# Up projections with the activations stationary, turned through memory and convolved a strip later

## The chip, the cores and the metric

The kernel runs on one core of a Trainium2 chip. The metric is the device time of one execution in microseconds (us), as a median over runs. Engines are named as in the profile: PE is TensorE's matmul and PEld its weight load, DVE is VectorE, ACT is ScalarE, POOL is GpSimd and SP is SyncE. Time in the trace counts from the first instruction of the profiled execution.

## What is computed

A decoder trunk of two layers on 256 tokens of width 2048. Each layer has attention, a gated feed-forward block with a short causal convolution, and a gated embedding that is added. The change lies in the feed-forward block:

```python
def causal_depthwise_conv(u, w, bias):      # width 3, each channel on its own
    ...
    return y + bias.astype(u.dtype)

def conv_ffn(h, w_up, conv_w, conv_b, w_down):
    u = causal_depthwise_conv(h @ w_up, conv_w, conv_b)
    gate, val = u[..., :D_FF], u[..., D_FF:]
    return (jax.nn.silu(gate) * val) @ w_down
```

`h` is 256 x 2048, `w_up` is 2048 x 11264 (D_FF is 5632) and `w_down` is 5632 x 2048. A token's convolved value takes in the two tokens before it, of the same channel. All data are float32; a product is made of three products of rounded parts, because each operand is split into a high part and the low rest (high x high, high x low, low x high).

## The kernel before

**Weights.** A weight matrix is cut into strips of 512 output columns. `weights` (L286) brings a strip in by SP's queue, 1 MB (four blocks of 128 rows) at a time, into four `raw` buffers, and splits two blocks at once: ACT writes the high part `whi` (L314), DVE the low part `wlo` (L315). Four `whi` and four `wlo` buffers exist, each for two blocks (a pair), so the split of a pair waits until PE has finished the pair four places earlier. An up strip has 16 blocks, which is 8 pairs.

**Two ways to multiply.** `strip_t` (L332) holds 128 x 128 pieces of the weights as the stationary operand and streams the activations. For each block and each of the strip's four groups of 128 channels it makes one matmul of 512 columns (the high weights by both parts of all 256 tokens, L341) and one of 256 columns (the low weights by the high part, L344). Its result lies in four PSUM banks with the channels on the partitions. `strip_v` (L347) holds 128 tokens of the activations as the stationary operand and streams the weights. For each block and each half of the tokens it makes three matmuls of 512 columns (L356 to L358). Its result lies in two PSUM banks with the tokens on the partitions. The banks come from a pool of five (`acc`). Both keep the last two blocks for the end, and then finish one bank after the other.

**The feed-forward block.** `ffn` (L617) calls `part` (L628) for 5 strip pairs, then the down projection of these with `strip_v` (`add_strips`, L595 to L615), then `part` for the other 6, and the down projection again. A strip pair is a strip of gates and the strip of values that they multiply: 22 up strips in each of two layers, 44 in all, each by `strip_t`. After a strip `conv` (L620) takes the four banks: `evac` (L361) adds the two halves of a bank on ACT and DVE (L363, L364) and multiplies by the norm's row `rstd` (L366); ACT scales by the third tap and adds the bias (L624); DVE adds the two other taps, shifted by one and by two tokens (L625, L626). Tokens lie along the free axis here, so a shift is a shift of addresses. Then SiLU on ACT for a gate (L636), or the product with the gate on DVE (L642) and the split into `g` (L152, L153) for a value. The parts `g` feed the down projection in the order of the strips.

**Turning.** The output projections of attention and the gated embeddings use `strip_v` as well and need their sums with channels on the partitions. For three strips of four `turn` (L242) does it: DVE transposes blocks of 32 x 32 (L250), POOL's queue writes them to a scratch tensor in device memory (`there`, L253) and reads them back in another order (`turned`, L257). It is used 15 times. The result has the shape 128 x 8 x 4 x 32: eight runs of 32 tokens for each of four channel groups. It has one buffer.

**Order.** The frame's scheduler puts each engine's instructions in order. `tc.high_priority` draws the weight splits ahead by a fixed distance, and `tc.issue_after` keeps one instruction behind another. Each engine runs its instructions strictly in that order, so one that waits holds all behind it.

Of the kernel before, what the change touches and what calls it, by code (L numbers as in the profile page):

```python
# [13 lines left out]
I32 = mybir.dt.int32  # L14
# [59 lines left out]
def tile_trunk(ctx, tc, head_d, xT_d, x_d, pT_d, pos_d, vec_d, cst_d, csb_d, wqkv, wo_a, wkv, wq_b, wo_b, wup, wdn, wpg, wpp, gfin_d, out_d):  # L74
# [133 lines left out]
    class Norm:  # L208
# [17 lines left out]
        def done(self, row=True):  # L226
# [6 lines left out]
            dg = tt("diag", tag="t", bufs=6)  # L233
# [8 lines left out]
    def turn(s):  # L242

        there = dram.tile([2 * P, 512], F32, tag="turn", name=nm("there"))
        for t in range(2):
            y = rt("y")
            nc.vector.transpose(  # L250
                y.rearrange("p (b o r) -> p o b r", b=4, o=4), strip_of(t, s).rearrange("p (o b c) -> p o b c", o=4, b=4)
            )
            nc.gpsimd.dma_start(there[t * P : (t + 1) * P], y)  # L253
        z = tt("turned", (P, 8, 4, 32), bufs=1)
        back = there.rearrange("(a c) (b f) -> b c a f", c=32, b=4)
        for b in range(4):
            nc.gpsimd.dma_start(z[32 * b : 32 * b + 32].rearrange("p a o r -> p a (o r)"), back[b])  # L257
        return [z[:, :, o] for o in range(4)]
# [27 lines left out]
    def weights(W, s, n, fine=False, before=lambda k0: None, block=None, base=0, ringed=0):  # L286

        size = 2 if fine else RAW
        for k0 in range(0, n, size):
# [8 lines left out]
            for i in range(0, w, 2):  # L298
# [11 lines left out]
                for c in (slice(0, 1), slice(1, 2)) if one else (slice(0, 2),):  # L310
                    r = raw[:, i + c.start : i + c.stop]
                    with tc.high_priority(offset=AHEAD):
                        with tc.issue_after(block(c.start)) if one else ExitStack():
                            last["high"] = nc.scalar.activation(hi[:, c], r, AF.Copy).ins  # L314
                        nc.vector.tensor_tensor(lo[:, c], r, f32(hi[:, c]), op=OP.subtract)  # L315
# [91 lines left out]
    def rotary_angles():  # L407
        pi = tt("posi", (ROT, S), I32, tag="t", bufs=6)
# [5 lines left out]
        n = tt("rn", (ROT, S), tag="t", bufs=6)  # L414
        nh = tt("rnh", (ROT, S), F32R, tag="t", bufs=6)
        nl = tt("rnl", (ROT, S), tag="t", bufs=6)
# [20 lines left out]
    def rotate(t):  # L437

        sw = tt("sw", (ROT, S), tag="t", bufs=6)
# [177 lines left out]
    def ffn(i, xs, rstd):  # L617
        cv = V_CONV + i * 4 * 2 * FB

        def conv(j, ps, y):  # L620
            col = lambda r: vec[:, cv + r * 2 * FB + j : cv + r * 2 * FB + j + 1]
            u = tt("u", tag="t", bufs=6)
            evac(ps, rstd, u)
            nc.scalar.activation(y, u, AF.Identity, scale=col(2), bias=col(3))  # L624
            nc.vector.scalar_tensor_tensor(y[:, 1:], u[:, : S - 1], col(1), y[:, 1:], op0=OP.mult, op1=OP.add)  # L625
            nc.vector.scalar_tensor_tensor(y[:, 2:], u[:, : S - 2], col(0), y[:, 2:], op0=OP.mult, op1=OP.add)  # L626

        def part(strips):  # L628
            gs = []
            for s in strips:  # L630
                ps = strip_t(wup[i], s, xs)
                gates = []
                for o in range(4):
                    y = tt("gate", bufs=4)
                    conv(4 * s + o, ps[o], y)
                    silu = nc.scalar.activation(y, y, AF.Silu).ins  # L636
                    gates.append(y)
                ps = strip_t(wup[i], FB // 4 + s, xs)
                for o in range(4):
                    y = tt("val", tag="t", bufs=6)  # L640
                    conv(FB + 4 * s + o, ps[o], y)
                    nc.vector.tensor_tensor(y, y, gates[o], op=OP.mult)  # L642
                    g = rt("g", dt=F32R)
                    split(y, g)
                    gs.append(g)
            return gs, silu
# [119 lines left out]
    for i in range(2):  # L766
        norm = Norm()
        h = add_strips(wo_a if i == 0 else wo_b, o, G_FFN + i * KB, norm)
        rstd, _ = norm.done()
        pb = p_blocks(i)  # L770
        h, norm = ffn(i, h, rstd)
# [93 lines left out]
```

## Time and profile before

| | |
|---|---|
| median of 3 runs | 2358.26 us (2357.72 to 2359.83) |
| profiled execution | 2358.29 us, of which the span from first to last instruction is 2356.5 us |
| PE busy | 2342.1 us (99%) in 12138 matmuls |
| DVE busy | 1578.5 us (67%) |
| ACT busy | 1270.9 us (54%) |
| POOL busy | 52.4 us (2%) |
| DMA | 458.55 MB, mean 195 GB/s |
| granted TensorE clock | 0.998 of full speed |

The span is the kernel, and what lies around it is 1.8 us. A busy share is that of a whole program with stages of different kinds, so the stage of the up strips is read by windows of its own. The end of a matmul in the trace is modelled, and matmuls overlap in it; the time that one takes is read from the distance between starts.

### The profile page before, as it was taken

Reading aid. Unit: us, or ns where it says so; the run is one execution under the profiler, and the core shown is the slowest. Engines: PE = TensorE matmul, PEld = TensorE weight load, DVE = VectorE, ACT = ScalarE, POOL = GpSimd, SP = SyncE. Lnnn points to the kernel's source line nnn. Section 1 sums busy time; section 2 is a strip of 40 time slices with the busy share of each in tenths; the row PEclk is TensorE's granted clock in tenths of the full one; section 3 lists DMA queues with packets and bytes.
Section 4 is the critical chain, followed back from the end, with each engine's and each line's share of the span. In section 5 each row is a group of like instructions: output and inputs, shape, how many; then the busy total and the mean of one; then the engine's idle time right before and its main releaser. Section 6 shows DMA issues by size and latency. Waiting matters only on the chain.

```text
span 2356.5 us, 31193 instructions
## 1 busy us (share of the span) xinstructions
PE 2342.1 (99%) x12138; PEld 1992.0 (85%) x12138; DVE 1578.5 (67%) x2407; ACT 1270.9 (54%) x1834; POOL 52.4 (2%) x94
## 2 busy tenths in 40 slices
PE   9999999999999999999999999999999999999998
PEld 7888888888888888888888888888888888888886
DVE  7566556778755777755668875677875577775555
ACT  6555545656534556545565444565653455654554
POOL 0000001000000000001010000100000000000100
PEclk9999999999999999999999999999999999999999
DMA  8455456555555555566565544665555555556663
GB/s 297 175 180 173 174 196 220 195 186 190 193 190 190 196 181 195 187 208 230 206 227 193 179 151 171 223 210 181 195 187 191 194 193 184 194 184 211 232 205 117
DMA packets 70133, 458.55 MB, mean 195 GB/s; under 512 B 8640, under 2 KB 9056, under 8 KB 18016
## 3 DMA queue, kind: packets, MB, share of 16 engines
q1 hardware_dynamic: 62352, 434.93, 52.9%
q0 software_dynamic: 5280, 15.73, 2.3%
q10 hardware_dynamic: 2352, 5.88, 0.7%
q8 instruction: 95, 1.56, 0.3%
q14 instruction: 54, 0.44, 0.1%
HBM read 446.56 MB, written 9.96 MB: 194 GB/s over the span
## 4 chain that ended last, share of the span: by engine, by line
PE 98%; DVE 1%; ACT 0%; DMA 0%; issue 0%; SPq 0%; DVEq 0%; ACTq 0%
PE acc L341 36%; PE acc L344 18%; PE accv L357 14%; PE accv L356 14%; PE accv L358 14%; PE two L385 2%; PE two L459 0%; DVE wlo L315 0%; DMA raw<-in_wqkv 0%; ACT whi L314 0%; PE keys L385 0%; PE two L460 0%; ACT sq L216 0%; PE two L267 0%; PE nrm L237 0%
## 5 line engine op out<-in xcount | busy, mean ns | idle before, releaser
L315 DVE TENSOR_TENSOR wlo<-raw,whi 128x1024 fp32r<-128x1024 f32 (+1 forms) x821 | 1002.1, 1221 | 698.2 <-ACT whi L314 694.2
L314 ACT ACTIVATE whi<-raw 128x1024 fp32r<-128x1024 f32 (+1 forms) x821 | 868.2, 1058 | 866.1 <-PE accv L358 425.7
L341 PE MATMUL acc<-h,whi 128*128 128x512 f32 x3712 | 1166.7, 396 | 2.1 <-DVE h L147 1.7
L344 PEld LDWEIGHTS acc<-h,wlo 128*128 128x128 f32 x3712 | 696.6, 188 | 163.9
L344 PE MATMUL acc<-h,wlo 128*128 128x256 f32 x3712 | 730.6, 278 | 0.0
L341 PEld LDWEIGHTS acc<-h,whi 128*128 128x128 f32 x3712 | 566.7, 189 | 5.0 <-DVE h L147 1.9
L356 PE MATMUL accv<-whi,g 128*128 128x512 f32 x704 | 273.9, 389 | 0.0
L357 PE MATMUL accv<-wlo,g 128*128 128x512 f32 x704 | 273.9, 389 | 0.0
L358 PE MATMUL accv<-whi,g 128*128 128x512 f32 x704 | 273.9, 389 | 0.0
L356 PE MATMUL accv<-whi,h 128*128 128x512 f32 x464 | 181.5, 391 | 0.0
L357 PE MATMUL accv<-wlo,h 128*128 128x512 f32 x464 | 181.2, 391 | 0.0
L358 PE MATMUL accv<-whi,h 128*128 128x512 f32 x464 | 181.2, 390 | 0.0
L358 PEld LDWEIGHTS accv<-whi,g 128*128 128x128 f32 x704 | 132.1, 188 | 27.4
L356 PEld LDWEIGHTS accv<-whi,g 128*128 128x128 f32 x704 | 132.1, 188 | 27.4
L357 PEld LDWEIGHTS accv<-wlo,g 128*128 128x128 f32 x704 | 132.1, 188 | 27.2
L363 ACT ACTIVATE c<-acc 128x256 f32<-128x256 f32 x232 | 86.2, 374 | 33.0 <-PE acc L344 32.9
L358 PEld LDWEIGHTS accv<-whi,h 128*128 128x128 f32 x464 | 87.1, 188 | 18.0
L356 PEld LDWEIGHTS accv<-whi,h 128*128 128x128 f32 x464 | 87.1, 188 | 17.7
L357 PEld LDWEIGHTS accv<-wlo,h 128*128 128x128 f32 x464 | 87.1, 188 | 17.4
L364 DVE TENSOR_TENSOR c<-acc,c 128x256 f32<-128x256 f32 x232 | 91.6, 415 | 0.0
L357 PE MATMUL accv<-wlo,o 128*128 128x512 f32 x224 | 87.4, 390 | 0.0
L358 PE MATMUL accv<-whi,o 128*128 128x512 f32 x224 | 87.3, 390 | 0.0
(184 smaller groups left out, 1457.7 us busy)
## 6 DMA issues: line engine op xcount, KB each, us to landing
raw<-in_wup SPq DMA_DIRECT2D x176, 1024.0 KB, 4.8
raw<-in_wdn SPq DMA_DIRECT2D x88, 1024.0 KB, 4.8
raw<-in_wqkv SPq DMA_DIRECT2D x44, 1024.0 KB, 4.8
raw<-in_wpg SPq DMA_DIRECT2D x32, 1024.0 KB, 5.1
raw<-in_wkv SPq DMA_DIRECT2D x24, 1024.0 KB, 4.8
raw<-in_wo_a SPq DMA_DIRECT2D x16, 1024.0 KB, 4.8
raw<-in_wq_b SPq DMA_DIRECT2D x12, 1024.0 KB, 4.9
raw<-in_wo_b SPq DMA_DIRECT2D x12, 1024.0 KB, 4.8
```

The lines of the kernel that those rows point to most:

```text
L314: last["high"] = nc.scalar.activation(hi[:, c], r, AF.Copy).ins
L315: nc.vector.tensor_tensor(lo[:, c], r, f32(hi[:, c]), op=OP.subtract)
L341: nc.tensor.matmul(ps[o], hi[:, c], xs[k], start=k == 0, stop=False)
L344: nc.tensor.matmul(ps[o][:, S:], lo[:, c], xs[k][:, :S], start=False, stop=k == n - 1)
L356: nc.tensor.matmul(ps[t], xl, hi, start=k == 0, stop=False)
L357: nc.tensor.matmul(ps[t], xh, lo, start=False, stop=False)
L358: nc.tensor.matmul(ps[t], xh, hi, start=False, stop=k == n - 1)
L363: last["copy"] = nc.scalar.activation(c, ps[:, S:], AF.Copy).ins
L364: last["sum"] = nc.vector.tensor_tensor(c, ps[:, :S], c, op=OP.add).ins
L385: run.append(nc.tensor.matmul(*args, skip_group_check=True, **kw).ins)
```

## The change

All up strips but the last value strip of each part go by `strip_v`: 9 of 10 strips in a first part and 11 of 12 in a second, 40 in the two layers. A strip's two banks are copied by ACT with the norm's column `rc` as scale (two copies of 128 x 512), transposed by DVE in 32 x 32 blocks, written to device memory and read back by POOL's queue. `turn` is cut for this into `turn_out` and `turn_in`. The convolution of a strip is issued one strip later, behind the next strip's copies and transposes. It works on runs of 32 tokens (`conv_turned`): for each channel group one ACT instruction and two DVE instructions inside the runs, then four small DVE instructions that carry the last one or two tokens of a run into the next. SiLU and the product with the gate are done for the four channel groups at once. The last value strip of a part stays with `strip_t` and the old `conv`; the gates of the same pair are convolved during it. Some buffers move: the transposes' output leaves the ring for the buffers `eh` and `el`, the tag `t` has 3 buffers and not 6, `gate` and `val` have one buffer of 128 x 4 x 256 each.

```diff
-    def turn(s):
+    def turn_out(strips):
         there = dram.tile([2 * P, 512], F32, tag="turn", name=nm("there"))
-        for t in range(2):
-            y = rt("y")
-            nc.vector.transpose(
-                y.rearrange("p (b o r) -> p o b r", b=4, o=4), strip_of(t, s).rearrange("p (o b c) -> p o b c", o=4, b=4)
-            )
+        for t, strip in enumerate(strips):
+            y = tt("y", (P, 768), tag=("eh", "el")[t], bufs=1)[:, :512]
+            last["turned"] = nc.vector.transpose(
+                y.rearrange("p (b o r) -> p o b r", b=4, o=4), strip.rearrange("p (o b c) -> p o b c", o=4, b=4)
+            ).ins
             nc.gpsimd.dma_start(there[t * P : (t + 1) * P], y)
+        return there
+
+    def turn_in(there):
         z = tt("turned", (P, 8, 4, 32), bufs=1)
         ...
+        def conv_turned(j, z, y):
+            runs = y.rearrange("p o (a r) -> p o a r", r=32)
+            for o in range(4):
+                nc.scalar.activation(runs[:, o], z[:, :, o], AF.Identity, scale=taps(2, j + o), bias=taps(3, j + o))
+                for d in (1, 2):
+                    c = runs[:, o, :, d:]
+                    nc.vector.scalar_tensor_tensor(c, z[:, :, o, : 32 - d], taps(2 - d, j + o), c, op0=OP.mult, op1=OP.add)
+            for d in (1, 2):
+                over = tt("over", (P, 7, 4, 2), bufs=2)[:, :, :, :d]
+                w = taps(2 - d, j, 4).unsqueeze(1).unsqueeze(3).to_broadcast([P, 7, 4, d])
+                nc.vector.tensor_tensor(over, z[:, :7, :, 32 - d :], w, op=OP.mult)
+                c = y.rearrange("p o (a r) -> p a o r", r=32)[:, 1:, :, :d]
+                nc.vector.tensor_tensor(c, c, over, op=OP.add)
         ...
             for s in strips:
-                ps = strip_t(wup[i], s, xs)
         ...
+                for value in (False, True):
+                    if value and s == strips[-1]:
+                        ps = strip_t(wup[i], FB // 4 + s, xs)
+                        with tc.issue_after(last["high"]), tc.issue_after(last["low weights"]):
+                            silu = finish_strip(waiting)
+                        y = room(True)
+                        for o in range(4):
+                            conv(FB + 4 * s + o, ps[o], y[:, o])
+                        values(y)
+                        continue
+                    ps = strip_v(wup[i], FB // 4 + s if value else s, xs)
+                    us = []
+                    for t in range(2):
+                        u = tt("u", (P, 768), tag="w", bufs=2)[:, :512]
+                        last["out"] = nc.scalar.activation(u, ps[t], AF.Copy, scale=rc[:, t : t + 1]).ins
+                        us.append(u)
+                    there = turn_out(us)
+                    if waiting is not None:
+                        with tc.issue_after(last["out"]), tc.issue_after(last["turned"]):
+                            finish_strip(waiting)
+                    z = turn_in(there)
+                    waiting = (value, s, z)
```

PE before, inside the first up strip of layer 0, the end of one pair of blocks and the start of the next (`acc` is one of the four banks, `h` a block of activations, `nrm` a small product of the norm):

```order
L341 MATMUL acc_3330<-h_2923,whi_3335 128x512
L344 MATMUL acc_3330<-h_2920,wlo_3336 128x256
L344 MATMUL acc_3330<-h_2923,wlo_3336 128x256
L341 MATMUL acc_3315<-h_3082,whi_3357 128x512
L341 MATMUL acc_3315<-h_3085,whi_3357 128x512
L344 MATMUL acc_3315<-h_3082,wlo_3358 128x256
L344 MATMUL acc_3315<-h_3085,wlo_3358 128x256
L341 MATMUL acc_3320<-h_3082,whi_3357 128x512
L341 MATMUL acc_3320<-h_3085,whi_3357 128x512
L237 MATMUL nrm_3297<-diag_3294,c_78 128x256
```

PE now, at the same place (`accv` is one of two banks):

```order
L362 MATMUL accv_3322<-wlo_3330,h_2923 128x512
L363 MATMUL accv_3322<-whi_3329,h_2923 128x512
L361 MATMUL accv_3315<-whi_3347,h_3082 128x512
L362 MATMUL accv_3315<-wlo_3348,h_3082 128x512
L363 MATMUL accv_3315<-whi_3347,h_3082 128x512
L361 MATMUL accv_3315<-whi_3347,h_3085 128x512
L362 MATMUL accv_3315<-wlo_3348,h_3085 128x512
L363 MATMUL accv_3315<-whi_3347,h_3085 128x512
L237 MATMUL nrm_3297<-diag_3294,c_78 128x256
```

A pair was 16 matmuls, 8 of 512 and 8 of 256 columns, and is 12 of 512; PE has 12012 rows before and 10732 now, 1280 fewer. The norm's product stands at the same depth of the strip, within the third pair.

DVE before, from the third weight pair of the strip that follows a gate strip (`c` and `u` are `evac`'s):

```order
L315 TENSOR_TENSOR wlo_3570<-raw_3567,whi_3569 128x1024
L364 TENSOR_TENSOR c_3483<-acc_3315,c_3483 128x256
L364 TENSOR_TENSOR c_3493<-acc_3320,c_3493 128x256
L366 TENSOR_TENSOR u_3482<-c_3483,rstd_3299 128x256
L366 TENSOR_TENSOR u_3492<-c_3493,rstd_3299 128x256
L364 TENSOR_TENSOR c_3503<-acc_3325,c_3503 128x256
L315 TENSOR_TENSOR wlo_3590<-raw_3567,whi_3589 128x1024
L625 SCALAR_TENSOR_TENSOR gate_3481<-u_3482,vec,gate_3481 128x255
L625 SCALAR_TENSOR_TENSOR gate_3491<-u_3492,vec,gate_3491 128x255
```

DVE now, from the third weight pair of the strip that follows a value strip: the transposes are of the strip just done, the convolution is of the gate strip before it:

```order
L320 TENSOR_TENSOR wlo_4036<-raw_4033,whi_4035 128x1024
L247 STREAM_TRANSPOSE y_3966<-u_3961 128x4x4x32
L320 TENSOR_TENSOR wlo_4052<-raw_4033,whi_4051 128x1024
L247 STREAM_TRANSPOSE y_3969<-u_3963 128x4x4x32
L643 SCALAR_TENSOR_TENSOR gate_3972<-turned_3818,vec,gate_3972 128x8x31 x2
L643 SCALAR_TENSOR_TENSOR gate_3972<-turned_3818,vec,gate_3972 128x8x30 x2
L320 TENSOR_TENSOR wlo_4070<-raw_4067,whi_4069 128x1024
L643 SCALAR_TENSOR_TENSOR gate_3972<-turned_3818,vec,gate_3972 128x8x31 x2
L643 SCALAR_TENSOR_TENSOR gate_3972<-turned_3818,vec,gate_3972 128x8x30
L320 TENSOR_TENSOR wlo_4086<-raw_4067,whi_4085 128x1024
L643 SCALAR_TENSOR_TENSOR gate_3972<-turned_3818,vec,gate_3972 128x8x30
L647 TENSOR_TENSOR over_3985<-turned_3818,vec 128x28
```

The sums and products of `evac` are gone from DVE. Two transposes stand in their place, and the convolution now stretches over three weight pairs, from the fourth to the sixth.

POOL now, within a part (before, POOL has no row between the two projections around a feed-forward block):

```order
L250 DMA there_3965<-y_3966 128x512
L250 DMA there_3965<-y_3969 128x512
L258 DMA turned_3992<-there_3965 32x8x128 x4
L250 DMA there_4139<-y_4140 128x512
L250 DMA there_4139<-y_4143 128x512
```

Each up strip now issues two writes and four reads there; a read of the one `turned` buffer stands behind the convolution that still uses it.

## Rows read from the trace of the kernel before

**Rows 1.** The page's head: span, and busy time, share and instructions by engine.

```profile
span 2356.5 us, 31193 instructions
PE 2342.1 (99%) x12138; PEld 1992.0 (85%) x12138; DVE 1578.5 (67%) x2407; ACT 1270.9 (54%) x1834; POOL 52.4 (2%) x94
```

**Rows 2.** The page's chain that ended last: shares of the span by engine.

```profile
PE 98%; DVE 1%; ACT 0%; DMA 0%; issue 0%; SPq 0%; DVEq 0%; ACTq 0%
```

**Rows 3.** Windows within layer 0's feed-forward block, and of two up strips.

```profile
core 0: us, PE busy (x) PEld busy (x) DVE busy (x) ACT busy (x) POOL busy (x), PEclk, DMA share, GB/s
420.00:900.00 480.00, 480.00 (x2613) 413.99 (x2612) 335.26 (x515) 262.40 (x376) 0.00 (x0) 1.00 0.54 189
...
462.22:506.81 44.59, 44.59 (x258) 38.91 (x257) 33.82 (x56) 26.13 (x42) 0.00 (x0) 1.00 0.54 189
```

**Rows 4.** Timeline of PE in an up strip: start, length, instruction, count.

```profile
425.01 0.63 PE L341 MATMUL acc<-h,whi 128*128 128x512 f32 x2
425.48 0.39 PE L344 MATMUL acc<-h,wlo 128*128 128x256 f32 x2
425.71 0.63 PE L341 MATMUL acc<-h,whi 128*128 128x512 f32 x2
```

**Rows 5.** Timeline of ACT: first copy from PSUM behind an up strip, two strips apart.

```profile
462.22 0.36 ACT L363 ACTIVATE c<-acc 128x256 f32<-128x256 f32 x1
...
506.81 0.36 ACT L363 ACTIVATE c<-acc 128x256 f32<-128x256 f32 x1
```

**Rows 6.** Timeline of PE in a strip of the down projection.

```profile
703.07 0.39 PE L356 MATMUL accv<-whi,g 128*128 128x512 f32 x1
703.29 0.39 PE L357 MATMUL accv<-wlo,g 128*128 128x512 f32 x1
...
703.75 0.39 PE L356 MATMUL accv<-whi,g 128*128 128x512 f32 x1
```

**Rows 7.** Timeline of DVE: sums behind two neighbouring 16-block strips of attention's output projection.

```profile
329.91 1.28 DVE L610 TENSOR_TENSOR x<-accv,x 128x512 f32<-128x512 f32 x2
...
351.67 1.28 DVE L610 TENSOR_TENSOR x<-accv,x 128x512 f32<-128x512 f32 x2
```

**Rows 8.** Groups by line: busy us, mean ns of one, idle before and releaser.

```profile
L315 DVE TENSOR_TENSOR wlo<-raw,whi 128x1024 fp32r<-128x1024 f32 (+1 forms) x821 | 1002.1, 1221 | 698.2 <-ACT whi L314 694.2 <-PE acc L341 0.5
...
L364 DVE TENSOR_TENSOR c<-acc,c 128x256 f32<-128x256 f32 x232 | 91.6, 415 | 0.0
...
L626 DVE SCALAR_TENSOR_TENSOR val<-u,vec,val 128x254 f32<-128x254 f32 x88 | 40.2, 477 | 0.8
...
L153 DVE TENSOR_TENSOR g<-val,g 128x256 fp32r<-128x256 f32 x88 | 36.8, 418 | 0.0
...
L147 DVE SCALAR_TENSOR_TENSOR h<-turned,vec,h 128x256 fp32r<-128x256 f32 x60 | 26.4, 482 | 10.8 <-ACT h L146 10.4
L250 DVE STREAM_TRANSPOSE y<-x 128x512 f32<-128x512 f32 x30 | 21.1, 702 | 0.0
...
L556 DVE TENSOR_SCALAR nmx<-mx 128x1 f32<-128x1 f32 x24 | 3.3, 149 | 0.0
```

**Rows 9.** Timeline of DVE where a part ends and the down projection begins.

```profile
618.35 1.23 DVE L315 TENSOR_TENSOR wlo<-raw,whi 128x1024 fp32r<-128x1024 f32 x1 [1.56 <-ACT whi L314]
...
632.67 1.22 DVE L315 TENSOR_TENSOR wlo<-raw,whi 128x1024 fp32r<-128x1024 f32 x1
```

**Rows 10.** A turn on POOL; then of all turns, issue times and time to landing.

```profile
359.30 0.57 POOL L253 DMA_DIRECT2D there<-y  x1 [16.15 <-DVE y L250]
...
366.65 2.34 POOL L257 DMA_DIRECT2D turned<-there  x4 [5.06 <-DMA there<-y]
...
L257 POOL DMA_DIRECT2D turned<-there x60: 582/592/611, 340.8 to 2231.1; - x60
...
DMA to landing us min/median/max: 2.8/4.5/8.0
```

**Rows 11.** The page's queue of POOL's DMAs: packets, MB, share of 16 engines' span.

```profile
q0 software_dynamic: 5280, 15.73, 2.3%
```

More of the change, by code (lines that the diff above doesn't have):

```diff
@@ L257, in turn @@
             nc.gpsimd.dma_start(z[32 * b : 32 * b + 32].rearrange("p a o r -> p a (o r)"), back[b])
+        return z
+    def turn(s):
+        z = turn_in(turn_out([strip_of(t, s) for t in range(2)]))
         return [z[:, :, o] for o in range(4)]
@@ L314, in weights @@
                             last["high"] = nc.scalar.activation(hi[:, c], r, AF.Copy).ins
-                        nc.vector.tensor_tensor(lo[:, c], r, f32(hi[:, c]), op=OP.subtract)
+                        last["low weights"] = nc.vector.tensor_tensor(lo[:, c], r, f32(hi[:, c]), op=OP.subtract).ins
                 yield k0 + i, [hi[:, c] for c in range(2)], [lo[:, c] for c in range(2)]
@@ L413, in rotary_angles @@
         nc.vector.tensor_scalar(r, r, c32[:ROT, C_FREQ : C_FREQ + 1], None, op0=OP.mult)
[L414 to L416 removed]
+        n = tt("rn", (ROT, S), tag="t", bufs=3)
+        nh = tt("rnh", (ROT, S), F32R, tag="t", bufs=3)
+        nl = tt("rnl", (ROT, S), tag="t", bufs=3)
         for parts in (PI_PARTS, PI_PARTS):
@@ L628, in part @@
         def part(strips):
             gs = []
-            for s in strips:
-                ps = strip_t(wup[i], s, xs)
[L632 to L645, printed above, removed]
+            gate = [None]
@@ new lines, in gates, with values, room @@
+            def gates(y):
+                silu = nc.scalar.activation(y, y, AF.Silu).ins
+                gate[0] = y
+                return silu
+            def values(y):
+                nc.vector.tensor_tensor(y, y, gate[0], op=OP.mult)
+                for o in range(4):
+                    g = rt("g", dt=F32R)
+                    split(y[:, o], g)
+                    gs.append(g)
+            def room(value):
+                return tt("val" if value else "gate", (P, 4, S), bufs=1)
@@ new lines, in finish_strip @@
+            def finish_strip(strip):
+                value, s, z = strip
+                y = room(value)
+                conv_turned(4 * s + (FB if value else 0), z, y)
+                return (values if value else gates)(y)
+            waiting = None
+            for s in strips:
+                for value in (False, True):
[4 more added lines that the diff above has]
+                        y = room(True)
+                        for o in range(4):
+                            conv(FB + 4 * s + o, ps[o], y[:, o])
[13 more added lines that the diff above has]
+                    waiting = (value, s, z)
@@ L768, in tile_trunk @@
         h = add_strips(wo_a if i == 0 else wo_b, o, G_FFN + i * KB, norm)
-        rstd, _ = norm.done()
+        rstd, rc = norm.done()
         pb = p_blocks(i)
-        h, norm = ffn(i, h, rstd)
+        h, norm = ffn(i, h, rstd, rc)
         _, rc = norm.done(row=False)
```

20 lines of the change are left out of this document (11 added, 9 removed).

## The prediction

> **What bounds the kernel now.** I read the page's head first, then the chain of waits, then windows of the stage that changes. PE is busy 99% of 2356.5 us [rows 1], and the chain that ended last lies on PE for 98% [rows 2]. A share over the whole span could hide a stage with another limit, so the windows decide: from 420 to 900 us, which holds up strips and down strips of layer 0, PE is busy 480.00 of 480.00 us, with a granted clock of 1.00, which is the upper level, 2.4 GHz [rows 3]. No other engine sets the pace there: over two up strips of 44.59 us DVE is busy 33.82 us (76%) and ACT 26.13 us (59%) [rows 3]. So the price of an edit in this stage is what it does to PE's own stream, as long as the weight splits on ACT and DVE stay ahead of PE.
>
> **What PE saves.** For one block an up strip by `strip_t` makes four matmuls of 512 columns and four of 256; `strip_v` makes six of 512. Both are 3072 columns, so a price by the column alone would give no gain. The starts tell otherwise. Two matmuls of 512 and two of 256 (1536 columns) take 425.71 - 425.01 = 0.70 us [rows 4], and three of 512 (also 1536 columns) take 703.75 - 703.07 = 0.68 us [rows 6]. The timeline rounds to 0.01 us, so I take the difference over whole strips. Two up strips are 506.81 - 462.22 = 44.59 us, 22.295 us each [rows 5]. A strip by `strip_v` with the same 16 blocks is 351.67 - 329.91 = 21.76 us [rows 7]. The gain is 0.535 us a strip, and 40 strips give 21.4 us. In the matmuls' terms: one of 512 columns takes 21.76 / 96 = 0.2267 us, and one of 512 with one of 256 takes 22.295 / 64 = 0.3484 us, so one of 256 takes 0.1217 us. Half the columns cost more than half the time; a straight line through both leaves 16.7 ns to each matmul whatever its columns, and a strip has 96 of them and not 128 (32 x 16.7 ns = 0.535 us).
>
> The Trainium skill speaks against this. TensorE: Matmul & The Clock Gate, section "Wait — 56ns, not 53.3ns?", puts back-to-back matmuls at N / 2.4 GHz plus about 2.5 ns. By that figure a strip would lose only 32 x 2.5 ns = 0.08 us, and 40 strips 3 us. The two strips measured here, at a granted clock of 1.00, differ by 0.535 us, so the trace does not agree for this kernel's operands.
>
> **What DVE gets and loses.** A gate strip costs DVE now 8 low splits (8 x 1.221) and for each of four channel groups a sum, a product of the same shape and two taps (4 x (0.415 + 0.415 + 0.477 + 0.477)), 16.9 us; a value strip has eight more of 0.418 us, 20.2 us [rows 8]. After the change a gate strip has the splits (9.77), two transposes (2 x 0.702), eight taps on runs and four small instructions. The taps on runs have a near row: the same operation reading the same turned shape, 0.482 us, against 0.477 us for whole rows [rows 8]; I take 0.482. The small ones (28 or 56 elements a partition) are not in the trace; 0.149 us (one element) and 0.477 us bound them, and I take 0.25, nearer to the short one [rows 8]. That is 9.77 + 1.40 + 3.86 + 1.00 = 16.0 us (15.6 to 16.9). A value strip adds one product of 1024 elements, for which the split of that size stands, 1.22, and four low parts, 1.67: 18.9 us (18.5 to 19.8). Both stay under 21.76 us, so DVE does not become the bound, and a strip pair costs it 34.9 us where it cost 37.1 (instructions overlap a little at their ends, so the window of a pair shows 33.82 us busy for these [rows 3]). ACT reads the same elements out of PSUM in two copies where it had four, and keeps a whole pass for the third tap and one for SiLU or the high part; its 59% stays about so.
>
> Order matters as well as the sum, since a low split behind the convolution is late. The four buffers put PE four pairs behind, each worth 21.76 / 8 = 2.72 us. The longest piece between two low splits is a transpose and four taps, 2.6 us, then three taps, then one tap with the small ones and the product, 2.7 us. With 1.5 us of slack a pair the lag grows to about 3 us, below the 8 us of three filled pairs. I cost it at nothing.
>
> **What the turn costs.** It is off PE's path, if it fits. It is now in a loop, since `turned` has one buffer: the reads for a strip wait until the convolution of the strip before has read its data, and the next convolution stands on ACT and DVE behind the next strip's copies, ahead of weight splits. The loop is the convolution's reading, stretched over three pairs (8.2 us), four issues (2.34 us) and a landing of 4.5 us [rows 10]: 15.0 us. The writes fit beside it: they begin with the transposes, and 359.30 to 366.65, 7.3 us, is the time from their first issue to the reads' issue where nothing else holds these [rows 10]. So the data lie there some 6.7 us before ACT asks for them. POOL is idle else. The transfers load the DMA engines: 15 turns took 2.3% of the span [rows 11], 3.6 us each, so one in 21.76 us adds 0.17 to a share of 0.54 [rows 3]; the weights' four `raw` buffers hold about 21 us of work, so I cost that at nothing too.
>
> **Where a part ends.** Four times the gates' convolution (3.86 + 1.00 us on DVE) falls beside the last value strip, just ahead of the old four-bank evacuation. Today the low splits there drift from 618.35 to 632.67, 14.32 us for five pairs where PE needs 5 x 2.72 = 13.60 [rows 9], 0.7 us late. With 4.9 us more the lag is 5.6 us, under the 8.2 us of filled pairs. I take nothing; if the taps on runs cost double, the lag is 9.5 us and PE waits 1.3 us, four times, 5 us. That is the upper bound.
>
> **The sum.** 2358.29 (the profiled execution; the median is 2358.26, so it stands for the runs) - 21.4 = 2336.9 us. Nothing else on PE changes: the norm's product stands at the same depth of the first strip, and the four last value strips are as before.
>
> **Rivals.**
> *No change, a matmul costs its columns.* If the 21.76 us belonged to the output projection's operands and an up strip by `strip_v` took its old 22.295 us, the time would stay at 2358.3. Against it: the down strips, with other operands, run at the same 0.68 us for three [rows 6]. Chance 0.04. The Trainium skill's section named above speaks for it, with 3 us of gain and so about 2355 us, which a measurement could not tell from no change.
> *Late weight splits.* The convolution is worse placed than I think, or runs are dear, and PE waits at the ends of parts and here and there inside: 5 to 10 us, 2342 to 2347. For it: the value strip leaves DVE only 2.9 us. Against it: it leaves less today, 22.3 - 20.2 = 2.1 us, and PE does not wait [rows 3]. Chance 0.08.
> *Slower, the turn's loop becomes the bound.* If each of POOL's four issues had to wait out a low split (0.592 + 1.221 us) and the landing took its longest, 8.0 us, the loop would be 8.2 + 7.3 + 8.0 = 23.5 us a strip [rows 8, 10]. ACT and DVE would stand at the convolution with the weight splits behind it, and PE would lose 1.7 us in 40 strips against 21.76: 2336.9 + 70 = 2407 us. It decides above 22.3 us, so with 7.3 us more than I expect. For it: DVE runs far more beside these issues than beside the old turns. Against it: issues that lay among the same splits never took over 0.611 us [rows 10]. Chance 0.04.
> The Trainium skill, SBUF — State Buffer, section "Who interferes with whom", says that GpSimd and DVE lock each other out of a shared port, in DVE's two-port modes or with two SBUF inputs against GpSimd's reads. That is the mechanism of this rival; the spread of 582 to 611 ns shows nothing of it so far.
>
> **How the numbers follow.** The forecast has 0.84, and its own uncertainty is small: the strip's gain is known to about 0.01 us (0.5 us in 40), runs differ by up to 1.6 us from their median, and the ends of parts cost 0 to 5 us. The range runs from 2336.9 - 2.4 to 2336.9 + 6.1, which takes in the start of the late splits: 2334.5 to 2343. About 0.2% (4.7 us) is what a measurement can tell from no change, so faster means under 2353.5. The forecast and the late splits are faster (0.92), the first rival is the same (0.04), the loop is slower (0.04).
>
> **What would show it.** In the profile after: about 10860 matmuls, 480 of 480 us still busy in a window of the up stage, strips 21.76 us apart, DVE near 80% in them. Waits of the weight splits should end on PE, as today. It would be wrong if ACT waits for `turned` data, if the issues of `turned` on POOL exceed 0.62 us, or if the low splits wait for the convolution and PE has gaps at strip ends or at the four part ends.

## The result, and the profile after the change

The changed kernel takes 2341.72 us (median; 2340.60 to 2342.63), the kernel before 2357.99 us beside it: a ratio of 0.993, with an interval of 0.9913 to 0.9947. That is 0.7% less, clear of the noise: faster, as forecast, and inside the range, but 4.8 us above the predicted 2336.9. The profiled execution took 2340.9 us, 17.4 us less than the 2358.29 of before, where 21.4 were counted.

The head of the page of after stands against [rows 1], its two lines of POOL's and of the instructions' queue against [rows 11], and its chain against [rows 2]:

```profile
span 2339.1 us, 28812 instructions
PE 2322.6 (99%) x10858; PEld 1935.8 (83%) x10858; DVE 1528.7 (65%) x2261; ACT 1254.1 (54%) x1688; POOL 191.6 (8%) x334
...
q0 software_dynamic: 19360, 57.69, 8.5%
...
q8 instruction: 85, 1.39, 0.2%
...
PE 97%; DVE 1%; DMA 1%; issue 0%; ACT 0%; POOL 0%; DVEq 0%; ACTq 0%
```

PE's matmuls fell from 12138 to 10858, its busy time by 19.5 us, and POOL's queue went from 2.3% to 8.5%. The bound is still PE. But DMA has 1% of a chain in which it had 0%, so somewhere PE now waits, through others, for a transfer. The windows tell where: the up stage, and then the four ends of parts, two in layer 0 (600 and 970) and two in layer 1 (1710 and 2080). Columns as in [rows 3]:

```profile
420.00:590.00 170.00, 170.00 (x752) 140.76 (x751) 117.83 (x177) 97.09 (x123) 27.38 (x48) 1.00 0.73 242
462.00:505.52 43.52, 43.52 (x194) 36.04 (x193) 31.41 (x50) 25.40 (x33) 6.95 (x12) 1.00 0.72 242
600.00:630.00 30.00, 28.59 (x147) 24.04 (x146) 24.50 (x47) 17.57 (x27) 2.36 (x4) 1.00 0.57 200
970.00:1000.00 30.00, 27.85 (x146) 23.53 (x146) 24.22 (x48) 17.59 (x27) 2.35 (x4) 1.00 0.57 195
1710.00:1740.00 30.00, 30.00 (x159) 25.70 (x158) 26.71 (x52) 18.64 (x29) 2.34 (x4) 1.00 0.64 217
2080.00:2110.00 30.00, 30.00 (x159) 25.68 (x158) 27.12 (x53) 18.62 (x29) 2.79 (x5) 1.00 0.65 213
```

Inside the up stage PE is busy 170.00 of 170.00 us. ACT's first copies behind two neighbouring up strips stand 482.98 - 461.22 = 21.76 us apart (22.295 by [rows 5]), and so do all 40 strips within their parts:

```profile
461.22 0.69 ACT L693 ACTIVATE u<-accv,rcol 128x512 f32<-128x512 f32 x1 [0.30 <-PE accv L363]
...
482.98 0.69 ACT L693 ACTIVATE u<-accv,rcol 128x512 f32<-128x512 f32 x1 [0.30 <-PE accv L363]
...
485.87 1.57 ACT L640 ACTIVATE gate<-turned,vec 128x256 f32<-128x256 f32 x3
```

So the 21.4 us were there, and what is missing lies at layer 0's two ends of parts. These are PE's two waits there, with the last matmul ahead of the first one:

```profile
616.36 0.39 PE L363 MATMUL accv<-whi,g 128*128 128x512 f32 x1
618.16 0.50 PE L361 MATMUL accv<-whi,g 128*128 128x512 f32 x1 [1.41 <-DVE c L369]
...
991.06 0.50 PE L361 MATMUL accv<-whi,g 128*128 128x512 f32 x1 [2.15 <-DVE c L369]
```

Matmuls of a stream without waits start 0.227 us apart, and here one starts 618.16 - 616.36 = 1.80 us after the other: 1.57 us lost, and some 2.3 us at the second place by the same reckoning. 21.4 - 3.9 = 17.5 us, against 17.4 measured. That leaves no loss of size on PE to explain.

**What PE waited for.** DVE's sum `c` at L369 (L364 before the change) is the second step of `evac`, which empties the last value strip's PSUM bank; the down strip needs that bank for the second half of its output. DVE and ACT around it, as timelines:

```profile
612.38 0.33 DVE L647 TENSOR_TENSOR over<-turned,vec 128x28 f32<-128x28 f32 x2 [3.23 <-DMA turned<-there]
...
617.70 0.41 DVE L369 TENSOR_TENSOR c<-acc,c 128x256 f32<-128x256 f32 x1
...
612.36 2.08 ACT L640 ACTIVATE gate<-turned,vec 128x256 f32<-128x256 f32 x4 [1.62 <-DMA turned<-there]
614.35 1.04 ACT L319 ACTIVATE whi<-raw 128x1024 fp32r<-128x1024 f32 x1
615.29 0.90 ACT L368 ACTIVATE c<-acc 128x256 f32<-128x256 f32 x3
```

Both engines stand at the first instruction that reads `turned` (DVE 3.23 us, ACT 1.62 us), and both work strictly in their order. Behind that instruction stand the weight splits and then the bank's copy (ACT, 615.29) and sum (DVE, 617.70). The matmul that wants the bank starts 0.05 us after the sum's end, at 618.16.

**Why the data were late there.** A strip's end is counted here, and in what follows, from ACT's first copy of it. Within a part, ACT comes to the convolution of a strip 485.87 - 461.22 = 24.7 us after that strip's end (the row of L640 above), and by the times to landing of its four reads the data are there 17.0 us after it. At an end of a part the convolution is issued inside the last value strip, so it is asked for sooner: DVE stands there from 612.38 - 3.23 = 609.15 us, 17.4 us after the gate strip's end at 591.78. In layer 1 that is just enough, in layer 0 not. POOL's timeline at the two part ends of layer 0 and the first of layer 1:

```profile
596.37 0.56 POOL L250 DMA_DIRECT2D there<-y  x1 [2.15 <-DVE y L247]
604.15 1.77 POOL L258 DMA_DIRECT2D turned<-there  x3 [7.22 <-ACT g L152]
607.10 0.59 POOL L258 DMA_DIRECT2D turned<-there  x1 [1.18 <-issue]
...
976.09 0.61 POOL L258 DMA_DIRECT2D turned<-there  x1 [7.01 <-ACT g L152]
978.16 1.74 POOL L258 DMA_DIRECT2D turned<-there  x3 [1.46 <-issue]
...
1709.43 0.56 POOL L250 DMA_DIRECT2D there<-y  x1 [2.15 <-DVE y L247]
1715.25 2.34 POOL L258 DMA_DIRECT2D turned<-there  x4 [5.26 <-DVE val L649]
```

From the second write to the first read it is 5.8 us in layer 1 and 7.8 us in layer 0. The write landed in 5.1 us in layer 1, where the reads stand behind the convolution that still reads `turned` (`val`), and in 7.0 us in layer 0, where the first read follows the landing by 0.8 us (the releaser named for it, `g`, is only the event that came last by the profile). The DMA view of 594 to 600 shows what else was in flight then (queue: packets, MB, share of 16 engines; then an issue with its KB and us to landing):

```profile
q8 instruction: 1, 0.02, 1.0%
...
raw<-in_wdn SPq DMA_DIRECT2D x1, 1024.0 KB, 7.3
```

One packet of `q8`, 16 KB of instructions for an engine (85 of them in the whole program, 1.39 MB), went beside the write, and the weights' load of that time took 7.3 us too (4.8 us is the median for `wdn`). At the second part end of layer 0 it was the same: one packet, a write of 7.0 us and a load of 7.2. The same view at 1707 to 1713 has no `q8` packet, and its write took 5.1 us. Over the 40 strips of after, 11 had such a fetch 3 to 5 us behind the strip's end, and in 6 of them the second write took over 5.6 us; of the 29 without one there, none did (5.3 at most).

A late write alone does not make the data late, though. In three of these six strips, all inside parts, a write of 6.9 or 7.0 us was followed by data 16.8 to 17.3 us after the strip's end, as usual. At the two part ends POOL also held between its reads, by 1.18 and 1.46 us, so the last read was issued 15.3 and 15.4 us after the strip's end (13.8 or 13.9 in those three). The last read of the first part end, all four reads of the strip that ended at 789.85, whose write was as late, and the issue of the weights' load nearest to the former:

```profile
DMA to landing us min/median/max: 5.2/5.2/5.2
...
802.00 2.34 POOL L258 DMA_DIRECT2D turned<-there  x4 [7.00 <-ACT g L152]
...
DMA to landing us min/median/max: 3.0/3.0/3.1
...
606.63 0.33 SPq L302 DMA_DIRECT2D raw<-in_wdn  x1
```

Over seven traces (after and experiments 1 to 6 below) 38 second writes of strips that are read back took over 5.6 us. In the 18 of these strips whose last read was issued by 14.2 us after the strip's end, the data were there by 18.7 us; in the 20 where it was issued at 14.5 us or later, they came at 20.5 to 23.4 us. The next 1 MB load of weights is issued at 14.6 to 15.2 us, and at the first part end it landed at 20.2 us and the last read at 20.5. That the late reads wait for this load would fit, but no run moves it, so it is not shown.

### The profile page after: what moved, and what is told of

The parts are those of the page before. It is cut to its first block, busy times and chain, and to the rows that moved or that the text cites. A ratio compares the mean times of both kernels' runs of the same rounds, so it can differ in the third digit from the quotient of the medians.

```text
span 2339.1 us, 28812 instructions
## 1 busy us (share of the span) xinstructions
PE 2322.6 (99%) x10858; PEld 1935.8 (83%) x10858; DVE 1528.7 (65%) x2261; ACT 1254.1 (54%) x1688; POOL 191.6 (8%) x334
## 3 DMA queue, kind: packets, MB, share of 16 engines
q8 instruction: 85, 1.39, 0.2%
## 4 chain that ended last, share of the span: by engine, by line
PE 97%; DVE 1%; DMA 1%; issue 0%; ACT 0%; POOL 0%; DVEq 0%; ACTq 0%
PE accv L361 26%; PE accv L363 26%; PE accv L362 26%; PE acc L346 10%; PE acc L349 5%; PE two L390 2%; DVE wlo L320 0%; DMA turned<-there 0%; PE two L464 0%; DVE val L643 0%; DVE gate L643 0%; PE keys L390 0%; PE two L272 0%; DMA vec<-in_head 0%; POOL turned L258 0%
## 5 line engine op out<-in xcount | busy, mean ns | idle before, releaser
L361 PE MATMUL accv<-whi,h 128*128 128x512 f32 x1744 | 679.8, 390 | 0.0
L363 PE MATMUL accv<-whi,h 128*128 128x512 f32 x1744 | 679.4, 390 | 0.0
L362 PE MATMUL accv<-wlo,h 128*128 128x512 f32 x1744 | 679.2, 389 | 0.0
L363 PEld LDWEIGHTS accv<-whi,h 128*128 128x128 f32 x1744 | 327.4, 188 | 68.1
L362 PEld LDWEIGHTS accv<-wlo,h 128*128 128x128 f32 x1744 | 327.5, 188 | 67.5
L361 PEld LDWEIGHTS accv<-whi,h 128*128 128x128 f32 x1744 | 327.5, 188 | 67.0
L346 PE MATMUL acc<-h,whi 128*128 128x512 f32 x1152 | 363.5, 397 | 0.7 <-DVE h L147 0.6
L349 PEld LDWEIGHTS acc<-h,wlo 128*128 128x128 f32 x1152 | 216.4, 189 | 50.6
L349 PE MATMUL acc<-h,wlo 128*128 128x256 f32 x1152 | 227.4, 279 | 0.0
L250 POOL DMA_DIRECT2D there<-y x110 | 62.4, 567 | 1711.4 <-DVE y L247 1703.3
L346 PEld LDWEIGHTS acc<-h,whi 128*128 128x128 f32 x1152 | 177.6, 190 | 3.3 <-ACT whi L319 1.5
L258 POOL DMA_DIRECT2D turned<-there x220 | 129.0, 593 | 306.6 <-DMA there<-y 88.5
```

The source lines that it names most:

```text
L346: nc.tensor.matmul(ps[o], hi[:, c], xs[k], start=k == 0, stop=False)
L349: nc.tensor.matmul(ps[o][:, S:], lo[:, c], xs[k][:, :S], start=False, stop=k == n - 1)
L361: nc.tensor.matmul(ps[t], xl, hi, start=k == 0, stop=False)
L362: nc.tensor.matmul(ps[t], xh, lo, start=False, stop=False)
L363: nc.tensor.matmul(ps[t], xh, hi, start=False, stop=k == n - 1)
```

## The experiments

Two theories of the part ends were to be told apart first. *Data*: PE waits because the turned data come late, where a fetch of instructions falls on the write. *Work* or *place*: the convolution's 4.9 us of DVE work there, or the place itself, makes the sums late.

**1. The last gate strip is not read back.** The convolution of a part's last gate strip has the same instructions, but on the data of the strip before.

```diff
+                    old = None if waiting is None else waiting[2]
...
-                    z = turn_in(there)
+                    z = old if s == strips[-1] else turn_in(there)
```

> In each part the last gate strip is written out but not read back; its convolution uses the data of the value strip before it, which lie in the buffer already. The instructions on VectorE and ScalarE are the same, so the output's gates of those four strips are left out. The changed kernel has two gaps of PE, 1.41 and 2.15 us, where layer 0's two parts end (3.9 us between starts). Theory 'data': VectorE and ScalarE stand there for the data of the last gate strip, and the sum that frees PE's bank stands behind them. Then both gaps go, and the span falls from 2339.1 by 3.9 to 2335.2 us. Theory 'work': the convolution's 4.9 us of VectorE work at that place makes the sum late. Then the gaps stay and the span stays at 2339.1 us.

It took 2335.98 us, with a span of 2334.2 us, 4.9 less than after (1.0 us of that lies at the start of the program, ahead of the up strips). The windows of layer 0's part ends:

```profile
600.00:630.00 30.00, 30.00 (x154) 25.48 (x153) 28.48 (x55) 19.96 (x32) 0.00 (x0) 1.00 0.52 183
970.00:1000.00 30.00, 30.00 (x155) 25.52 (x154) 28.53 (x56) 20.36 (x33) 0.00 (x0) 1.00 0.53 184
```

DVE is busier in 600 to 630 than in after (28.48 against 24.50 us), and PE has no gap, though the second writes were late there too (7.5 and 6.9 us). It is the wait for data, not the work.

**2. The fetches are moved.** 32 matmuls of 128 columns into an unread bank go ahead of layer 0's up strips; the rest is unchanged. The 85 packets of `q8` come to one for every 255 of PE's rows, matmuls and weight loads, so they should be PE's; the places where a block of its instructions is fetched then fall elsewhere.

```diff
+        if i == 0:
+            pad = bank("pad")
+            for _ in range(32):
+                nc.tensor.matmul(pad[:, :P], IDB, IDB, start=True, stop=True)
```

> 32 more matmuls of 128 columns before layer 0's up strips, into a bank that nobody reads; PE's stream of instructions is 64 longer from there, so the 16 KB fetches of instructions (one for 256 instructions) come a third of an up strip earlier, some 7 us. Theory 'fetch': at layer 0's part ends the fetch 4.15 us behind the strip's end delays the second write to memory (7.0 us to landing and not 5.0) and with it the data (20.5 and 21.3 us behind the strip's end and not 17.1). Then the fetch lies 3 us ahead of the strip's end, the data land at about 17.1 us, both gaps go, and the span is 2339.1 - 3.9 + the 32 matmuls (about 2) = 2337 us. Rival 'place': something else at layer 0's part ends is slow there (the weights' own transfers, the part's first down strip). Then the data stay at 20 to 21 us, the gaps stay, and the span is about 2341 us.

2337.88 us, span 2336.1 us. No fetch fell within 3 to 5 us behind the last gate strips of layer 0; their data landed 17.0 and 17.2 us after the strips' ends, and the gaps are gone:

```profile
600.00:630.00 30.00, 30.00 (x156) 25.57 (x156) 26.18 (x51) 18.43 (x28) 2.36 (x4) 1.00 0.61 213
970.00:1000.00 30.00, 30.00 (x157) 25.60 (x157) 26.43 (x52) 19.38 (x29) 2.35 (x4) 1.00 0.62 218
```

So the place alone does not do it: POOL's holds between the reads are at both ends as before, but behind writes of 5.3 and 5.2 us. Three strips inside this run's parts did get their data 20.7 to 22.8 us after their end, each with a fetch beside it, and there PE lost nothing: within a part ACT asks for them after 24.7 us. This is one execution, and it ties the delay to the fetch; it does not show how the one holds up the other.

**3. DVE's order alone.** If the data may be late, the bank should be emptied before the engines stand at the convolution. This version issues the gates' convolution behind the first bank's sum.

```diff
-                        with tc.issue_after(last["high"]), tc.issue_after(last["low weights"]):
-                            silu = finish_strip(waiting)
                         y = room(True)
                         for o in range(4):
                             conv(FB + 4 * s + o, ps[o], y[:, o])
+                            if o == 0:
+                                with tc.issue_after(last["sum"]):
+                                    silu = finish_strip(waiting)
```

> The last gates of a part are convolved behind the first bank's sum of the last value strip, no longer ahead of it; all work is kept. Theory 'data' and theory 'work' both say that the bank comes free in time: no gaps at the part ends, span 2335.2 us, median about 2337.8 us, ratio to the kernel before 0.9914. If the convolution then comes too late for the down projection (its last four blocks are needed 21.8 us after the up strips' end in a first part), gaps of 1 to 3 us stand before the ninth pair of the first down strip, and the gain is smaller.

A miss: 2339.77 us (2335.93 to 2341.56), a ratio of 0.9918 (0.9904 to 0.9932), and in the profiled execution PE still waited 2.14 and 1.54 us for the same sum. The timelines of ACT, then of DVE, tell why:

```profile
613.22 2.08 ACT L640 ACTIVATE gate<-turned,vec 128x256 f32<-128x256 f32 x4 [3.48 <-DMA turned<-there]
616.16 0.90 ACT L368 ACTIVATE c<-acc 128x256 f32<-128x256 f32 x3
...
616.28 1.23 DVE L320 TENSOR_TENSOR wlo<-raw,whi 128x1024 fp32r<-128x1024 f32 x1 [5.28 <-ACT whi L319]
617.43 0.42 DVE L369 TENSOR_TENSOR c<-acc,c 128x256 f32<-128x256 f32 x1
```

DVE no longer waits for `turned`, but ACT does, and on ACT the four passes of the convolution stayed ahead of the bank's copy. DVE stood 5.28 us for ACT instead. The wait had two engines, and I had moved one.

**4. The last pair by the old way.** The last gate strip of each part goes through `strip_t` again, as the last value strip does, so nothing at a part's end reads turned data. 36 strips keep the change.

```diff
-                    if value and s == strips[-1]:
-                        ps = strip_t(wup[i], FB // 4 + s, xs)
...
+                    if s == strips[-1]:
+                        ps = strip_t(wup[i], FB // 4 + s if value else s, xs)
...
```

> One part undone: the last gate strip of each part is multiplied with the weights stationary and convolved the old way, so 36 strips and not 40 go the new way. Strip price: 4 x 0.535 = 2.1 us lost. Theories 'data' and 'work': no turned strip is waited for at the part end, so the two gaps (3.9 us) go: span 2339.1 + 2.1 - 3.9 = 2337.3, median about 2340. If the gaps came from the old evacuation of the last value strip itself, they stay: 2341.2, median about 2344.

2340.05 us (2339.33 to 2340.61), a ratio of 0.9924 (0.991 to 0.9938); span 2337.9 us with PE busy in all of 600 to 630 and 970 to 1000. The gaps are gone, and four strips at the old price (4 x 0.535 = 2.1 us) are paid for it. The theory of the data gives this, and so does that of the work; what it excludes is that the old evacuation of the last value strip makes the gaps by itself.

**5. Both engines' order.** As the third, and ACT's passes too stand behind its copy of the first bank.

```diff
+                            if o == 0:
+                                with tc.issue_after(last["copy"]), tc.issue_after(last["sum"]):
+                                    silu = finish_strip(waiting)
```

> As e3_gates_behind_sum, but the last gates are issued behind the first bank's copy on ScalarE as well as behind its sum on VectorE. In e3 ScalarE still had the four first taps of the gates ahead of the bank's copy and stood 3.5 us for the data there. Theory 'data' (what stands behind an instruction that waits for the turned data is late): with nothing that frees the bank behind such an instruction, no gap at the four part ends, span 2335.2 us, median 2337 us, and runs that lie closer together than e3's 2335.9 to 2341.6. Theory 'work': the gates' 4.9 us still lie there, gaps of 1.4 to 2.1 us stay, span 2338 to 2339 us.

2336.07 us (2336.03 to 2336.24; before beside it 2357.81), a ratio of 0.9905 (0.989 to 0.992). The profile of this run has a late write as well, so its good time isn't luck. POOL, ACT and DVE at the first part end, then the windows:

```profile
595.52 0.56 POOL L250 DMA_DIRECT2D there<-y  x1 [2.14 <-DMA there<-y]
602.80 1.76 POOL L258 DMA_DIRECT2D turned<-there  x3 [6.73 <-DVE val L662]
...
612.52 0.36 ACT L368 ACTIVATE c<-acc 128x256 f32<-128x256 f32 x1
612.78 2.07 ACT L640 ACTIVATE gate<-turned,vec 128x256 f32<-128x256 f32 x4
...
613.79 0.42 DVE L369 TENSOR_TENSOR c<-acc,c 128x256 f32<-128x256 f32 x1
...
600.00:630.00 30.00, 30.00 (x153) 25.50 (x152) 25.32 (x50) 18.74 (x28) 2.36 (x4) 1.00 0.59 199
970.00:1000.00 30.00, 30.00 (x154) 25.54 (x153) 25.34 (x50) 19.22 (x29) 2.35 (x4) 1.00 0.59 200
```

The second write to the first read is 7.3 us here (7.8 in after), POOL's hold is there, and the data came 20.6 us after the strip's end at the first part end and 21.8 at the second, as late as in after. But ACT copies the bank before it comes to `turned`, and by then, 21.9 us after the strip's end, the data are there. This version beats both kernels: 21.7 us under before, where the strips' price gives 21.4, and 7.0 us under the changed kernel beside it (experiment 6).

**6. The changed kernel once more.** Nothing is edited, and it ran beside the fifth.

> The changed kernel once more, beside e5 on the same chip: median 2341.7 us by its first four runs, with two gaps at layer 0's part ends. If the fetch of instructions that delays the turn collides by chance, the runs differ by some 2 us from each other.

2343.05 us (2339.91 to 2344.34), a ratio of 0.9932 (0.992 to 0.9944). Five times of one kernel spread over 4.4 us, the fifth version's four over 0.2 us. In the profiled execution the first part end had no gap (a second write of 5.7 us, and data 16.7 us after the strip's end), and the second a longer one, of 2.93 us (7.3 and 22.0 us). Then this, on PE, and in a window of the same stretch:

```profile
990.45 0.80 PE L361 MATMUL accv<-whi,g 128*128 128x512 f32 x1 [2.93 <-DVE c L369]
991.04 0.63 PE L362 MATMUL accv<-wlo,g 128*128 128x512 f32 x1
...
990.00:997.00 7.00, 6.55 (x16) 5.15 (x17) 6.20 (x15) 3.53 (x5) 0.00 (x0) 0.52 0.48 163
```

Behind the gap the matmuls start 0.43 us apart, not 0.227, and the granted clock of the window is 0.52, the lower level, 1.2 GHz. 16 matmuls, each 0.20 us longer, lose some 3 us more: the wait was paid twice. In after, gaps of 1.41 and 2.15 us left the clock at 1.00.

**7. The price of a matmul.** Of each three matmuls in the 40 strips the second and third are cut in two halves of 256 columns: the same columns, 64 matmuls more in a strip.

```diff
-            nc.tensor.matmul(ps[t], xh, lo, start=False, stop=False)
-            nc.tensor.matmul(ps[t], xh, hi, start=False, stop=k == n - 1)
+            for w in (lo, hi):
+                for c in (slice(0, S), slice(S, 2 * S)) if halves else (slice(0, 2 * S),):
+                    nc.tensor.matmul(ps[t][:, c], xh, w[:, c], start=False, ...)
...
-                    ps = strip_v(wup[i], FB // 4 + s if value else s, xs)
+                    ps = strip_v(wup[i], FB // 4 + s if value else s, xs, halves=True)
```

> In the 40 strips the second and third matmul of each three (the low weights and the high weights by the activations' high part) are cut into two of 256 columns each: the columns stay 49152 a strip, the matmuls rise from 96 to 160. By the line through the two kinds of strip (16.7 ns a matmul whatever its columns) a strip rises by 64 x 0.0167 = 1.07 us to 22.83 us, and 40 strips by 43 us: 2382 us. By a fixed cost of 2.5 ns, as the Trainium skill's TensorE: Matmul & The Clock Gate has it, a strip rises by 0.16 us to 21.92 us and the kernel by 6.4 us: 2347 us. The first is the theory that the gain was counted by, the second its rival.

2376.25 us, span 2374.4 us. ACT's first copies behind two neighbouring strips:

```profile
463.69 0.69 ACT L694 ACTIVATE u<-accv,rcol 128x512 f32<-128x512 f32 x1 [0.36 <-PE accv L364]
...
486.44 0.69 ACT L694 ACTIVATE u<-accv,rcol 128x512 f32<-128x512 f32 x1 [0.36 <-PE accv L364]
```

22.75 us a strip, 0.99 more than in after; by 64 that is 15.5 ns for each added matmul. The line through the strips of [rows 5, 7] had said 16.7. The change had saved 32 matmuls a strip and this adds 64, and the time follows their number: a matmul's price beside its columns is real here. Every matmul of this kernel comes with a weight load of its own (as many PEld as PE on every page), so these runs can't tell whether the price is the matmul's or the load's.

The Trainium skill, TensorE: Matmul & The Clock Gate, section "Wait — 56ns, not 53.3ns?", gives about 2.5 ns as a matmul's fixed cost; an estimate by it is 40 x 64 x 2.5 ns = 6 us more than after. The span grew by 35 us, and by 39 beside an after without its gaps, of which this run has none at the part ends. The measurement decides against the page's figure for these operands.

**8. No deferral.** The convolution is issued behind its own strip's turn and not one strip later.

```diff
-                        with tc.issue_after(last["high"]), tc.issue_after(last["low weights"]):
-                            silu = finish_strip(waiting)
...
-                    if waiting is not None:
-                        with tc.issue_after(last["out"]), tc.issue_after(last["turned"]):
-                            finish_strip(waiting)
                     z = turn_in(there)
-                    waiting = (value, s, z)
+                    with tc.issue_after(last["out"]), tc.issue_after(last["turned"]):
+                        silu = finish_strip((value, s, z))
```

> One part undone: the convolution of a strip is issued behind its own turn and not one strip later; the scheduler puts it six or seven weight pairs on. It asks for the data some 15 us behind the strip's end, and they land at 17, in the strips that a fetch hits at 18 to 22. Theory 'reserve': the filled pairs (8 us) cover a wait of 2 us each strip and PE has no gaps but in two or three strips that a fetch hits late; span 2335 to 2342 us. Theory 'deferral is what hides the turn': ScalarE and VectorE stand 2 us in each strip with the weight splits behind them and the lag adds up; PE loses 1 us or more a strip, 40 to 80 us in all, 2375 us or more.

2496.55 us, span 2494.7 us. The page's row of engines and its chain, the largest group of waits for `turned` (us in total, times, longest), and one such wait on ACT:

```profile
PE 2378.0 (95%) x10858; PEld 1962.3 (79%) x10858; DVE 1520.8 (61%) x2261; ACT 1238.5 (50%) x1688; POOL 191.3 (8%) x334
...
PE 60%; DMA 18%; DVE 11%; issue 5%; POOL 3%; ACT 1%; POOLq 0%; DVEq 0%; SPq 0%; ACTq 0%
...
DVE over L647 <- DMA turned<-there: 313.7, 40, 12.4
...
512.58 2.08 ACT L640 ACTIVATE val<-turned,vec 128x256 f32<-128x256 f32 x4 [10.34 <-DMA turned<-there]
```

The same work costs 155.6 us more than in after: 100 us in which PE is idle (116.7 against 16.5), and 55 in which the same matmuls took longer, since the granted clock was at 0.5, the lower level, in about 125 us (by the run's mean of 0.975; about 10 us in after, by 0.998). In each strip DVE waits some 8 us for `turned` with the weight splits behind it. So the strip of deferral is what hides the turn. The second theory holds, but its 40 to 80 us were too few: in the row above ACT asks at 512.58 - 10.34 = 502.24, which is 11.0 us after that strip's end (491.25) and not some 15, and the data come 21.3 us after it and not 17.

## Why the prediction came out as it did

- **What bounds the kernel, and what PE saves:** right. 10858 matmuls where about 10860 were named, strips 21.76 us apart, 170.00 of 170.00 us busy; with the part ends mended, the whole gain is 21.7 us where 21.4 were counted (experiment 5). The price by the matmul, worked out from whole strips, was borne out by experiment 7 (15.5 ns for 16.7). The rival that a matmul costs its columns fell with it.
- **What DVE gets and loses:** right, by smaller numbers. Taps on runs took 0.46 us (0.482 taken), the small products 0.20 and their additions 0.20 to 0.22 (0.25 taken), the long product 1.22 as taken. "DVE near 80%" was wrong by its own rows: 34.9 us for a pair was a sum of single durations, and [rows 3] had shown that 37.1 of these fill 33.8 us of a window. By that share 34.9 give 31.8, and 31.41 of 43.52 us (72%) were measured.
- **What the turn costs:** right within a part. A DMA share of 0.17 more was forecast, 0.18 or 0.19 came (0.72 to 0.73 for 0.54); the data lie there 24.7 - 17.0 = 7.7 us before ACT asks (6.7 forecast). POOL's issues took 582 to 612 ns, under the 0.62 that was named as the limit, so the slower rival did not come. What it feared would cost dearly, as experiment 8 shows: where ACT and DVE do stand at the convolution in every strip, the time is 2496.55 us. But there too the issues took 582 to 612 ns, so its cause, issues that wait out a low split, occurred in no run.

The page SBUF — State Buffer of the Trainium skill, section "Who interferes with whom", states a lock on a port that GpSimd and DVE share. These issues show no sign of it: beside a DVE that is 72% busy they stayed at 582 to 612 ns.

- **Where a part ends:** this is the step that failed. I asked how much work the convolution adds there (4.9 us, a lag of 5.6 under a cover of 8.2) and took nothing for it, and that held: experiment 1 has all of the work and no gap. I did not ask when its data come. The 6.7 us of reserve were worked out for a convolution behind the next strip's copies, and at a part's end it stands ahead of the last strip's evacuation, so the reserve there is 17.4 - 17.0, nearly nothing, and at two of the four ends the data came 20.5 and 21.3 us after the strip's end. The loss, 3.9 us in the profiled execution, lies within the bound of 5 us, but that bound was for another mechanism and held by chance.
- **The rival of late weight splits** gave 2342 to 2347 us, where the time nearly came out. Its mechanism didn't occur: PE waited for no weight split at the part ends but for a bank, and inside the parts not at all.
- **What would show it wrong** named it: "ACT waits for `turned` data", and PE gaps at part ends. Both are there, at two of four.

Open stays why only about half of the fetches that fall on a second write delay it: over the seven traces 37 of 70 writes with a fetch 3 to 5 us behind the strip's end took over 5.6 us, up to 8.3. Nor is it settled what POOL's hold of 1.18 and 1.46 us between its reads is. It stands at the same reads of layer 0's part ends in every one of these traces that has them, also in experiment 2 and at the first part end of experiment 6, where the data came at the usual time.

## What to carry to other kernels

Swapping which operand stays put can pay though the columns are the same, if it makes fewer matmuls; read the price of one from two shapes in the trace. A trip through memory that is hidden by issuing its consumer a stage later must be hidden at the stage's ends as well, where that consumer usually comes sooner, and with some microseconds to spare for a transfer that is late. On engines that work in order, put whatever frees a buffer for the bounding engine ahead of the first instruction that waits for a transfer, on every engine that takes part in freeing it.

## What was not expected of the hardware

- Beside a fetch of 16 KB of an engine's own instructions about half of the 256 KB writes took longer (37 of 70): 7.0 us and not 5.1 at the two part ends, where a 1 MB load took 7.2 and 7.3 us and not 4.8.
- Behind such a late write the last read decided: issued by 14.2 us after the strip's end, the data were there by 18.7 us; issued at 14.5 us or later, not before 20.5.
- With the engines' order as changed, the same kernel's runs spread over 4.4 us; with that of experiment 5, over 0.2 us.
- Each added matmul, with its weight load, cost 15.5 ns beside its columns, at a granted clock of 1.00.
- After a gap of 2.93 us in which PE waited, the granted clock was at the lower level for 6.8 us; after one of 2.15 us it stayed at the upper.
